# Making the first group of a max-unpooling kernel one image at a time

## The chip, the cores and the metric

The kernel runs on one core of a Trainium2 chip. The metric is the device time of one execution in microseconds (us), the median of several runs.

## The reference

A 2x2 max-unpooling: every input element goes to one of the four places of its 2x2 output block, chosen by an index from 0 to 3; the other three places are zero.

```
x: float32 [16, 64, 32, 32];  indices: int [16, 64, 32, 32], values 0..3
output[b, c, 2*i + idx // 2, 2*j + idx % 2] = x[b, c, i, j]     # else 0
```

The indices arrive as 64-bit integers, so the core reads 4.2 MB of x and 8.4 MB of indices and writes 16.8 MB.

## The kernel before

The 1,024 images lie on 128 partitions, eight images (t = 0..7) on each. Two images make a group; there are four groups, and each group is one store of 4 MiB. SyncE issues three loads, all on one queue: indices of images 0 to 2, all of x, indices of images 3 to 7. It then issues the four stores as VectorE signals them.

VectorE makes a piece of output with four instructions, one for each place in the 2x2 block: (index equals place) times x. Where it can, it treats two images in one instruction; images 2 and 3 are treated singly, because image 3 needs the second load of indices.

```
for t in range(T):                       # T = 8, G = 2, NG = 4, FIRST = 3
    g, k = t // G, t % G
    if t in (0, FIRST):
        ...                              # wait for this half of the indices
    if k == 1 and t != FIRST:
        continue
    n = 1 if k == 1 or t + 1 == FIRST else 2        # images per instruction
    if g == NG - 1:
        nc.vector.wait_ge(stored_0, 16)...          # group 3 reuses group 0's buffer
    ...
    for pidx in range(4):
        op = nc.vector.scalar_tensor_tensor(
            out=o_c[:, k : k + n, :, pidx // 2, :, pidx % 2],
            in0=idx_c[:, t : t + n], scalar=pidx, in1=x_c[:, t : t + n],
            op0=is_equal, op1=mult)
    if k + n == G:
        op.then_inc(made, 1)             # the group is made

for g in range(NG):
    nc.sync.wait_ge(made, g + 1)
    nc.sync.dma_start(out=out_v[g], in_=out_t[g]).then_inc(...)
```

Of the kernel before, what the change touches and what calls it, by code (L numbers as in the profile page):

```python
# [1 line left out]

# [4 lines left out]

P = 128
F32 = mybir.dt.float32
I32 = mybir.dt.int32  # L10


class Program:




    def __init__(self, nc):
        self.nc = nc
        self.block = nc.main_func.blocks[0]  # L20
        self.kernel_block = nc.cur_bb.bb.name

    def __enter__(self):
        ins = self.block.instructions
        self.branches = [i for i in ins if "Branch" in type(i).__name__]
        n = len(ins) - len(self.branches)
        assert all("Branch" in type(ins[k]).__name__ for k in range(n, len(ins)))
        del ins[n:]
        self.nc.switch_bb(self.block.name, parent=None)
        self.symbolic = self.nc._always_lower_symbolic_ap  # L30
        self.nc._always_lower_symbolic_ap = False
        return self

    def first(self, made):
        ins = self.block.instructions
        assert ins[len(ins) - 1].name == made.ins.name
        moved = ins.pop()
        at = next(
            k
            for k, i in enumerate(ins)  # L40
            if i.engine == moved.engine and isinstance(i, mybir.InstDrain)
        )
        ins.insert(at, moved)

    def last(self, made):


        def move(nc):
            ins = self.block.instructions
            at = next(k for k, i in enumerate(ins) if i.name == made.ins.name)  # L50
            nc.main_func.blocks[-1].instructions.append(ins.pop(at))

        self.nc.at_finalize(move)

    def __exit__(self, kind, *_):
        self.nc._always_lower_symbolic_ap = self.symbolic
        if kind is None:
            for b in self.branches:
                self.block.instructions.append(b)
            self.nc.switch_bb(self.kernel_block, parent=None)  # L60


@with_exitstack
def kernel(
    ctx: ExitStack,
    tc: tile.TileContext,
    x: bass.AP,
    indices: bass.AP,
    kernel_size: bass.AP,
    out: bass.AP,  # L70
):
    nc = tc.nc
    assert kernel_size == 2

    B, C, H, W = x.shape
    n_img = B * C
    T = n_img // P
    assert T * P == n_img and C % T == 0

    G = 2  # L80
    NG = T // G
    FIRST = 3
    N = H * W
    x_v = x.rearrange("b (ch t) h w -> (b ch) (t h w)", t=T)
    idx_v = indices.rearrange("b (ch t) h w -> (b ch) (t h w)", t=T).bitcast(I32)
    out_v = out.rearrange("b (ch g t) oh ow -> g (b ch) (t oh ow)", g=NG, t=G)

    x_t = nc.alloc_sbuf_tensor("x_t", [P, T * N], F32).ap()
    idx_t = nc.alloc_sbuf_tensor("idx_t", [P, T * 2 * N], I32).ap()
    out_t = [  # L90
        nc.alloc_sbuf_tensor(f"out_t{g}", [P, G * 4 * N], F32).ap()
        for g in range(NG - 1)
    ]
    out_t.append(out_t[0])

    x_in = nc.alloc_semaphore("x_in")
    idx_in = [nc.alloc_semaphore(f"idx_in{g}") for g in range(2)]
    made = nc.alloc_semaphore("made")
    stored_0 = nc.alloc_semaphore("stored_0")
    stored = nc.alloc_semaphore("stored")  # L100

    x_c = x_t.rearrange("p (t i j) -> p t i j", t=T, j=W)
    idx_c = idx_t.rearrange("p (t i j two) -> p t i j two", t=T, j=W, two=2)[
        :, :, :, :, 0
    ]
    cut = FIRST * 2 * N

    with Program(nc) as program:
        program.first(
            nc.sync.dma_start(out=idx_t[:, :cut], in_=idx_v[:, :cut]).then_inc(  # L110
                idx_in[0], 16
            )
        )
        program.first(nc.sync.dma_start(out=x_t, in_=x_v).then_inc(x_in, 16))
        program.first(
            nc.sync.dma_start(out=idx_t[:, cut:], in_=idx_v[:, cut:]).then_inc(
                idx_in[1], 16
            )
        )

        nc.vector.wait_ge(x_in, 16).then_inc(x_in, -16)
        for t in range(T):
            g, k = t // G, t % G
            if t in (0, FIRST):
                half = int(t == FIRST)
                nc.vector.wait_ge(idx_in[half], 16).then_inc(idx_in[half], -16)  # L126

            if k == 1 and t != FIRST:
                continue
            n = 1 if k == 1 or t + 1 == FIRST else 2  # L130
            if g == NG - 1:
                nc.vector.wait_ge(stored_0, 16).then_inc(stored_0, -16)
            o_c = out_t[g].rearrange(
                "p (m i two j wo) -> p m i two j wo", m=G, two=2, wo=2, j=W
# [4 lines that stand above are left out]
                    in0=idx_c[:, t : t + n],  # L139
                    scalar=pidx,  # L140
                    in1=x_c[:, t : t + n],
                    op0=mybir.AluOpType.is_equal,
                    op1=mybir.AluOpType.mult,
                )
            if k + n == G:
                op.then_inc(made, 1)

        for g in range(NG):
            nc.sync.wait_ge(made, g + 1)
            nc.sync.dma_start(out=out_v[g], in_=out_t[g]).then_inc(  # L150
                stored if g else stored_0, 16
            )
        nc.sync.sem_inc(made, -NG)
        program.last(
            nc.sync.wait_ge(stored, 16 * (NG - 1)).then_inc(stored, -16 * (NG - 1))
        )


# [1 line left out]
_INS = ['x', 'indices', 'kernel_size']  # L160
_OUTS = [((16, 64, 64, 64), 'float32')]

_NUMBERS = {'kernel_size': 2}


# [26 lines left out]
```

## Time and profile before

| | before |
|---|---|
| time, median of the first three runs | 71.51 us (71.4 to 71.56) |
| profiled span | 70.5 us |
| VectorE busy | 35.6 us, 20 instructions |
| transfer queue busy | 97.4% of 16 engines' span |
| first store issued | 28.60 us |
| first store packets start | 30.5 to 31.5 us |

The store is issued well before an engine can start on it, because each engine is still busy with load packets.

### The profile page before, as it was taken

What the parts mean: (1) busy time and instruction counts of PE and PEld (TensorE: products, weight loads), DVE (VectorE), ACT (ScalarE), POOL (GpSimd) and SP (SyncE); (2) the same over time, 40 slices, a digit from 0 to 9 for tenths busy, and PEclk for the clock granted to TensorE, in tenths of its full rate; (3) what the DMA queues carried; (4) which work ended last, traced back from release to release, by engine and by line L of the source; (5) the groups of instructions that cost most, each with busy time, mean ns of one, the idle gap of its engine ahead of it and who ended that gap; (6) DMA issues with size and microseconds to landing.
All of it is one profiled execution on the core that took longest, in us unless ns stands there. A gap on an engine that the chain in (4) does not pass through costs nothing.

```text
span 70.5 us, 72 instructions
## 1 busy us (share of the span) xinstructions
DVE 35.6 (51%) x20; POOL 0.2 (0%) x4
## 2 busy tenths in 40 slices
DVE  0000000000089999999999999999999300000000
POOL 1000000000000000000000000000000000000000
DMA  8799997979988999869898999989898989999891
GB/s 223 307 432 418 423 558 316 558 335 558 409 372 372 488 581 418 372 298 539 353 539 353 484 409 409 465 353 502 353 539 353 539 353 484 409 391 484 372 484 56
DMA packets 1008, 29.36 MB, mean 417 GB/s; under 512 B 112, under 2 KB 112, under 8 KB 112
## 3 DMA queue, kind: packets, MB, share of 16 engines
q1 hardware_dynamic: 1008, 29.36, 97.4%
HBM read 12.58 MB, written 16.78 MB: 417 GB/s over the span
## 4 chain that ended last, share of the span: by engine, by line
DVE 46%; DVEq 4%; issue 1%
DVE out_t L137 46%; DVEq L187 4%
## 5 line engine op out<-in xcount | busy, mean ns | idle before, releaser
L137 DVE SCALAR_TENSOR_TENSOR out_t<-idx_t,x_t 128x2048 f32<-128x2048 int32 (+1 forms) x20 | 35.6, 1860 | 19.7 <-DVEq L126 19.7
L173 POOL MEMSET const-bfloat16-1.0<- 128x1 bf16 x1 | 0.1, 103 | 0.0
L173 POOL MEMSET const-uint8-127<- 128x1 uint8 x1 | 0.1, 103 | 0.0
L173 POOL MEMSET const-float32-1.0<- 128x1 f32 x1 | 0.1, 100 | 0.0
L173 POOL MEMSET const-float32-0.0<- 128x1 f32 x1 | 0.1, 99 | 0.2 <-issue 0.2
## 6 DMA issues: line engine op xcount, KB each, us to landing
out_dram<-out_t SPq DMA_DIRECT2D x4, 4096.0 KB, 13.8
idx_t<-in_indices_dram SPq DMA_DIRECT2D x1, 5120.0 KB, 30.8
x_t<-in_x_dram SPq DMA_DIRECT2D x1, 4096.0 KB, 19.0
idx_t<-in_indices_dram SPq DMA_DIRECT2D x1, 3072.0 KB, 9.7
```

The costliest lines, as they stand in the source:

```text
L137: op = nc.vector.scalar_tensor_tensor(out=o_c[:, k : k + n, :, pidx // 2, :, pidx % 2], in0=idx_c[:, t : t + n], scalar=pidx, in1=x_c[:, t ...
L173: nc = _bacc.Bacc("TRN2", target_bir_lowering=False, num_devices=1)
L187: with _tile.TileContext(nc) as tc:
```

## The change

VectorE makes images 0 and 1 one after the other, as it does images 2 and 3. The diff isolates one effect: smaller instructions at the head of the work, and so a later issue of the first store.

```diff
-            if k == 1 and t != FIRST:
+
+            if k == 1 and t != FIRST and g:
                 continue
-            n = 1 if k == 1 or t + 1 == FIRST else 2
+            n = 1 if k == 1 or t + 1 == FIRST or not g else 2
```

## The prediction

> **What bounds the kernel now.** I read the views in this order: the page, to see which unit is full; the groups by shape, to get the price of one VectorE instruction; the chain of waits, to see when transfers land; and the trace cut into half-microsecond windows, to see whether the transfer engines ever lack work around the first store.
>
> The page of the kernel before:
>
> ```profile
> span 70.5 us, 72 instructions
> ...
> DVE 35.6 (51%) x20; POOL 0.2 (0%) x4
> ...
> DMA  8799997979988999869898999989898989999891
> ...
> q1 hardware_dynamic: 1008, 29.36, 97.4%
> HBM read 12.58 MB, written 16.78 MB: 417 GB/s over the span
> ```
>
> The reader should see that VectorE is busy for half of the span while the one transfer queue keeps 16 engines busy for 97.4% of it. The bytes are fixed by the problem: 12.58 MB in, 16.78 MB out. The first engine starts about 1 us after the first issue, so hardly any time is left in which the transfer engines are idle. The digits of the DMA row dip in places, but packets of this queue are 24 to 40 KB and are booked where they start, so single low digits are no proof of a gap. I need the waits for that.
>
> The chain of waits of the kernel before (start, length, what):
>
> ```profile
> 19.59 0.08 issue
> 19.67 12.07 DVE out_t L137 x7
> 31.74 0.15 issue
> 31.89 9.57 DVE out_t L137 x7
> 41.46 0.22 issue
> 41.69 2.57 DVEq L187
> 44.26 11.01 DVE out_t L137 x5
> ```
>
> This chain is VectorE's, but its breaks tell when transfers landed. At 19.6 x and the first three index images are there. At 31.7 VectorE resumes after its wait for the second part of the indices: the list of issues gives that load 30.8 us to landing, and it was issued at 0.90, so it landed at 31.7. At 41.4 comes the wait for the first store: the shortest issue-to-landing time of a store is 12.8 us, and 28.60 + 12.8 = 41.4. From the last load's landing to the first store's landing there are 9.7 us. A store is 4,096 KB, 4.19 MB; at 432 GB/s (what the windows show between 19.5 and 28.6, where the queue is certainly full) that is 9.7 us. So **there is no bubble between the last load and the first store**. Three more stores of 9.7 us from 41.4 give 70.5, the span. The whole kernel is about one microsecond of start and one uninterrupted string of transfers; VectorE runs beside it.
>
> The windows around the first store (window, length, DVE busy, POOL busy, clock, DMA share, GB/s), and the issue itself from the timeline:
>
> ```profile
> 29.50:30.00 0.50, 0.50 (x2) 0.00 (x0) 1.00 0.42 164
> 30.00:30.50 0.50, 0.50 (x1) 0.00 (x0) 1.00 0.00 0
> 30.50:31.00 0.50, 0.50 (x2) 0.00 (x0) 1.00 1.99 852
> 31.00:31.50 0.50, 0.50 (x1) 0.00 (x0) 1.00 0.46 197
> ...
> 28.60 0.35 SPq L150 DMA_DIRECT2D out_dram<-out_t  x1
> ```
>
> 852 GB/s in 0.5 us is 426 KB, which is 13 packets of 32 KB; 197 GB/s is 3 more. A row of out_t for two images is 32 KB, so these are the first store packets of all 16 engines: 13 start between 30.5 and 31.0, three between 31.0 and 31.5. The store was issued at 28.60. It therefore **sat in the queue for about 1.9 us or more**, behind the last load's 40 KB packets. That waiting time is what the change may eat.
>
> **What the Trainium skill says.** "VectorE: DVE Perf Modes", section on the TRN2 errata, says that instructions reading SBUF pay a fixed cost each, whatever their size, and gives (N+151)/0.96 ns for an fp32 instruction with two inputs: 2291 ns for 2048 elements, and 1224 for 1024. The trace agrees: 2286 and 1220 ns. "DMA: Bandwidth & Descriptors", section on queues, rings and completion order, says each engine consumes a queue's descriptors in ring order; the trace agrees, since a store issued at 28.60 starts only when the loads end. "Perfetto Trace Analysis", section on the HWDGE DMA instruction, says that the profiled window of such an instruction covers the issuing and not the movement of data; here the issue shows 0.35 us and the landing comes 12.8 us after its start.
>
> **The change part by part.** The loop now treats images 0 and 1 of group 0 one at a time. *Removed:* four instructions over 2048 elements. *Added:* eight over 1024. Groups 1 to 3 are made as before, and the signal for the first store still comes only with the last instruction of image 1, since it is given when k + n reaches 2. No bytes, buffers or transfers change. No wait is added: the second image needs nothing that the first did not.
>
> The cost comes from start-to-start distances, since successive VectorE records overlap a little at their ends. Two-image instructions: the timeline has the first at 19.67 and the third at 24.08, so 2.20 us each. One-image instructions: one starts at 31.89 in the chain, and the fourth after it (the last for image 3) at 36.43 in the timeline, so 4.54 us for four steps, 1.135 each. The groups by shape show the durations:
>
> ```profile
> L137 DVE SCALAR_TENSOR_TENSOR out_t<-idx_t,x_t 128x2048 f32<-128x2048 int32 x12 | 26.6, 2286 | 19.7 <-DVEq L126 19.7
> L137 DVE SCALAR_TENSOR_TENSOR out_t<-idx_t,x_t 128x1024 f32<-128x1024 int32 x8 | 9.2, 1220 | 0.0
> ```
>
> Group 0 now takes 8 x 1.135 = 9.08 us in place of 4 x 2.20 = 8.81, so **+0.28 us** on VectorE (four more fixed costs of 0.07 us). The first store is issued at 28.60 + 0.28 = 28.88 instead of 28.60.
>
> Does that reach the end? The deadline is the moment when the earliest engine runs out of load packets, between 30.5 and 31.0, less the time from an issue to the first packet. That time I take from the program's start: the first load is issued at 0.00, and the windows show no data in the first microsecond and full traffic in the second, so 1.0 us for the first engine; I allow 1.5 for the last. The store must be issued by about 30.5 - 1.5 = 29.0 at the most cautious, and by 29.5 at the likely figure. 28.88 meets both. The slack shrinks from about 0.9 to about 0.6 us by the likely figure. **The whole 0.28 us lies in the queue's waiting time: cost 0.**
>
> Later stores have more room. Store 1 is issued at 37.68 (timeline) and store 0 ends its transfer near 41.4, which leaves 3.7 us minus the 1.0 of issue; store 2 at 46.49 against 51.1; store 3 at 55.30 against 60.8. A shift of 0.28 in each changes nothing. VectorE even loses part of the shift, because it waits for the first store's landing at 41.4, which does not move, though it reaches this wait only just before that; I do not count on it. The sum is 71.5 + 0.0.
>
> **Rivals.** *First: the delay is passed on in full.* If the queue needs its descriptors earlier than I think (say 2 us before an engine runs dry, which no row here excludes for a store that reads SBUF), the 16 engines idle for up to 0.28 us between the last load and the first store, and every later landing shifts with it: 71.5 + 0.28 = 71.8, or +0.4%. Against it: before the change no time is lost at that joint, and the only issue latency on view is 1.0 us. *Second: VectorE becomes the bound.* It would have to lose the spare 2.7 to 4.5 us ahead of stores 1 to 3; 0.28 is too small. This would cost 0 as well. *Third: a gain.* Smaller instructions could finish an image earlier, but the store still waits for both, and the transfer queue is full anyway; nothing for it. *Fourth: VectorE's smaller instructions or a changed phase disturb the transfers.* Reads of SBUF by the store start while VectorE writes, as before; the engines move 431 to 446 GB/s in windows with either shape of instruction, so I see no effect of the shape.
>
> **How the range follows.** The best estimate is the median of before, 71.5. Its own three runs span 71.4 to 71.56; another chip or day may add a tenth or two on either side. The first rival adds 0.28 at about one chance in seven. The range is 71.3 to 71.8. Faster by over 2% would need 1.4 us out of a full queue: chance 0.01. Slower by over 2% would need five times the whole added VectorE time: 0.01. Within 2%: 0.98.
>
> **What would show each step right or wrong.** In the changed kernel the page should have 24 VectorE instructions, 16 of them over 1024 elements at about 1220 ns and 8 over 2048 at 2286, with VectorE busy near 35.9 us. The first store's issue should stand at about 28.9. The first store packets should still start in 30.5 to 31.5, with the issue-to-landing minimum down from 12.8 to about 12.5 us, and the chain should show the wait for the first store ending at 41.4 to 41.5 again. If instead that wait ends 0.2 us or more later while the last load still lands at 31.7, the store came too late for the queue and the first rival is right. The prediction would be wrong altogether if the one-image instructions were much dearer than 1.135 us when they are first on fresh data, or if the loads themselves ended earlier than in this trace, so that the slack was less than one profile shows.

## More of the kernel before

One reading aid for later: in a window, the DMA share books a packet's whole time where it starts. When each of the 16 engines starts exactly one packet in a window of 1 us, the DMA share is therefore the mean length of that packet in us.

## The result, and the profile after

| | before | after |
|---|---|---|
| time, median of six runs | 71.49 us (71.4 to 71.7) | 71.50 us (71.4 to 71.62) |
| ratio | | 0.9998 (95%: 0.9981 to 1.0015) |
| VectorE busy | 35.6 us | 35.9 us |
| x there, VectorE starts | 19.67 us | 19.56 us |
| first store issued | 28.60 us | 28.76 us |

A ratio is the mean time of one kernel's fast runs over that of the other's of the same rounds, so it is not quite the ratio of the medians quoted.

The page of the changed kernel, in the lines that answer to those of before:

```profile
span 70.2 us, 76 instructions
...
DVE 35.9 (51%) x24; POOL 0.2 (0%) x4
...
q1 hardware_dynamic: 1008, 29.36, 97.6%
```

The four more instructions and the 0.3 us of VectorE are there, and the queue is as full as before. The groups of the changed kernel by shape (busy us, then mean ns of one):

```profile
L138 DVE SCALAR_TENSOR_TENSOR out_t<-idx_t,x_t 128x1024 f32<-128x1024 int32 x16 | 18.3, 1219 | 19.6 <-DVEq L126 19.6
L138 DVE SCALAR_TENSOR_TENSOR out_t<-idx_t,x_t 128x2048 f32<-128x2048 int32 x8 | 17.7, 2283 | 0.0
```

The durations are those of before. The chain of waits of the changed kernel (start, length, what), up to the first store's landing:

```profile
19.56 11.92 DVE out_t L138 x11
31.48 0.57 issue
32.05 9.12 DVE out_t L138 x7
41.17 0.22 issue
```

The last load's landing is at 31.48 and the first store's at 41.17, 9.7 us apart, as before. (Both stand 0.26 to 0.29 us earlier than in the profile of before. That is not a gain of the change: VectorE's start, which the change cannot touch, is also earlier by 0.1, the profiled execution of before was 0.3 us over its median, and the timed runs of both kernels agree.) The issue of the first store (start, length, instruction; SPq is SyncE's queue), and the windows at the joint of loads and store, in the changed kernel:

```profile
28.76 0.35 SPq L151 DMA_DIRECT2D out_dram<-out_t  x1
...
30.50:31.00 0.50, 0.50 (x2) 0.00 (x0) 1.00 2.29 983
31.00:31.50 0.50, 0.50 (x2) 0.00 (x0) 1.00 0.15 66
```

983 GB/s in 0.5 us is 15 packets of 32 KB. All engines but one pass from loads to the store between 30.5 and 31.0, as soon as the loads end. VectorE's part from its start to the issue grew from 28.60 - 19.67 = 8.93 to 28.76 - 19.56 = 9.20 us, so by 0.27; all of it disappeared in the queue's waiting time.

### The profile page after: what moved, and what is told of

It is laid out like the page before. It is cut to its first block, busy times and chain, and to the rows that moved or that the text cites. A ratio compares the mean times of both kernels' runs of the same rounds, so it can differ in the third digit from the quotient of the medians.

```text
span 70.2 us, 76 instructions
## 1 busy us (share of the span) xinstructions
DVE 35.9 (51%) x24; POOL 0.2 (0%) x4
## 4 chain that ended last, share of the span: by engine, by line
DVE 46%; DVEq 4%; issue 1%
DVE out_t L138 46%; DVEq L188 4%
## 5 line engine op out<-in xcount | busy, mean ns | idle before, releaser
L138 DVE SCALAR_TENSOR_TENSOR out_t<-idx_t,x_t 128x1024 f32<-128x1024 int32 (+1 forms) x24 | 35.9, 1574 | 19.6 <-DVEq L126 19.6
## 6 DMA issues: line engine op xcount, KB each, us to landing
idx_t<-in_indices_dram SPq DMA_DIRECT2D x1, 5120.0 KB, 30.5
```

The lines of the kernel that those rows point to most:

```text
L138: op = nc.vector.scalar_tensor_tensor(out=o_c[:, k : k + n, :, pidx // 2, :, pidx % 2], in0=idx_c[:, t : t + n], scalar=pidx, in1=x_c[:, t ...
```

## The experiments

The time is the same, so the question is what makes it so: how much later could the store come, and does its issue matter at all? My theory was that each engine passes from its last load packet to its first store packet without a gap, as long as the store is issued some time ahead; beyond that each microsecond of delay costs one. The rivals were a queue that wants its work much earlier, and a time that does not depend on this issue at all. Each of the three calls of four runs shared its runs of the kernel before: 71.52, 71.49 and 71.50 us.

### Only the signal later, by one, two and three instructions

VectorE's work stays as it was before the change. Only the signal for group 0 moves onto an instruction of image 2 (number 1, 2 or 3), which is a clean dial for the issue time.

```diff
+                if (t, pidx) == (2, 0):          # (2, 1), (2, 2)
+                    op.then_inc(made, 1)
-            if k + n == G:
+            if k + n == G and g != 0:
                 op.then_inc(made, 1)
```

> The kernel before, with its ten or so microseconds of VectorE work unchanged; only the signal for the first store is moved from the last instruction of group 0 to the first instruction of image 2. The store is issued at about 28.60 + 1.14 = 29.73 us. Theory (the store has to be issued 1.0 to 1.5 us before an engine runs out of load packets, 30.6 to 31.4 us): this is just past the deadline, so the first engines stand idle; time +0 to +0.4 us (71.5 to 71.9). Rival 1 (the queue needs descriptors some 2 us ahead): +0.8 us or more. Rival 2 (the issue time of the first store is of no account within microseconds): +0.0.

> As the run before it, the signal two instructions later: the store is issued at about 30.87 us, when the first engines have run dry. Theory: the store packets can start only at 31.9 to 32.4, so the wait for the first store ends at about 42.4 instead of 41.4 and the time is 72.4 to 72.7 us (+0.9 to +1.2). Rival 1: +1.9 or more. Rival 2: +0.0 to +0.2.

> The kernel before with the signal for the first store three instructions later: issue at about 32.0 us. Theory (deadline 29.87, slope 1): +2.1 us, 73.6, slower by about 3%. Rival (only the step over the deadline costs, by a restart of the engines, not the length of the delay): +1.0 as in the run with the signal two later.

Measured: one later 71.58 us (ratio 1.0008, 0.9995 to 1.0022), two later 72.51 us (1.0139, 1.0125 to 1.0153), three later 73.68 us (1.0305, 1.0291 to 1.0319). The issue and the windows, first with the signal one later:

```profile
29.62 0.35 SPq L152 DMA_DIRECT2D out_dram<-out_t  x1
...
30.50:31.00 0.50, 0.50 (x2) 0.00 (x0) 1.00 2.29 983
```

Then with the signal two later:

```profile
30.86 0.35 SPq L152 DMA_DIRECT2D out_dram<-out_t  x1
...
30.50:31.00 0.50, 0.50 (x2) 0.00 (x0) 1.00 0.02 0
31.00:31.50 0.50, 0.50 (x1) 0.00 (x0) 1.00 0.00 0
31.50:32.00 0.50, 0.50 (x2) 0.00 (x0) 1.00 2.44 1049
```

And three later:

```profile
32.01 0.35 SPq L152 DMA_DIRECT2D out_dram<-out_t  x1
...
31.50:32.00 0.50, 0.50 (x2) 0.00 (x0) 1.00 0.00 0
32.00:32.50 0.50, 0.50 (x1) 0.00 (x0) 1.00 0.00 0
32.50:33.00 0.50, 0.50 (x1) 0.00 (x0) 1.00 2.43 1049
```

With the issue at 29.62 the engines still change over at the end of the loads. At 30.86 they have nothing to start between 30.5 and 31.5, and then all 16 start at once (1049 GB/s in half a microsecond is 16 packets). From issue to first packet that is 0.64 to 1.14 us by one run and 0.49 to 0.99 by the other. The single packets, which the kept traces hold though no view lists them, narrow it (windows of 0.05 us agree): the first engine starts 0.85 us after the issue and the last 1.0 us after it, with the signal two later as with three. The losses, 0.99 us at 30.86 and 2.19 at 32.01, grow by 1.20 for 1.15 us of delay. So the joint has a deadline near 30.86 - 0.99 = 29.87 us, and past it the loss follows the delay one for one. Both rivals fall: the issue time counts, and 2 us of lead are not needed. My own expectation of the first run was too pessimistic in its upper half; the lead of 0.85 to 1.0 us is shorter than the 1.0 to 1.5 us I had taken from the start of the program.

### The change carried further: half and quarter images

```diff
-            for pidx in range(4):
+            R = H if g else H // 2                # or H // 4
+            for pidx, r in [(p, r) for p in range(4) for r in range(0, H, R)]:
                 op = nc.vector.scalar_tensor_tensor(
-                    out=o_c[:, k : k + n, :, pidx // 2, :, pidx % 2],
+                    out=o_c[:, k : k + n, r : r + R, pidx // 2, :, pidx % 2],
                     ...                           # in0, in1 with r : r + R too
```

> The change carried one step further: group 0 in half images, 16 instructions over 512 elements. From the fixed cost of 0.07 us each, one takes 0.60 us and the group 9.63 instead of 8.81: the first store is issued at about 29.4 us, +0.83. Theory: at the likely deadline of 29.5, so +0.0 to +0.2 us. Rival 1 (2 us ahead): +0.5 or more. Rival 3 (many small instructions are dearer than the fixed cost says): the issue comes later than 29.6.

> The change carried further still: group 0 in quarter images, 32 instructions over 256 elements. Fixed cost 0.07 us each: 0.336 us from start to start, 10.75 us for the group, so the first store is issued at about 30.4 us. Theory after the first four runs (issues up to 29.6 are free; the run with the issue at 30.86 lost 0.99 us, so the joint's deadline is 30.86 - 0.99 = 29.87, and beyond it each microsecond of delay is one of time): +0.5 to +0.65 us (72.0 to 72.2). Rival (the issue time does not count, the loss of that run had another cause): +0.0.

Measured: halves 71.49 us (0.9999, 0.9987 to 1.0012), with the store issued at 29.52; quarters 72.26 us (1.011, 1.0096 to 1.0124). The issue with quarters, and the joint:

```profile
30.37 0.35 SPq L152 DMA_DIRECT2D out_dram<-out_t  x1
...
30.50:31.00 0.50, 0.50 (x1) 0.00 (x0) 1.00 0.02 0
31.00:31.50 0.50, 0.50 (x2) 0.00 (x0) 1.00 2.43 1049
```

Halves put the issue off by 0.92 us (0.82 counted from VectorE's start, which was 0.1 us later in this profile) and are still free. Quarters pass the deadline, the engines stand idle until 31.0, and the time grows. So the very thing that the change does has a cost, once there is enough of it. The size was a miss: 0.77 us against 0.5 to 0.65. Of this, 0.15 us is not in the span: for this kernel the time is 1.43 to 1.51 us longer than the span, against 1.27 to 1.38 for the others. The span itself grew by about 0.6 us, close to the 0.50 of the rule (30.37 - 29.87). What the extra time outside the span is was not tested; this kernel has the most instructions (100 in all).

### All groups one image at a time

```diff
-            if k == 1 and t != FIRST:
-                continue
-            n = 1 if k == 1 or t + 1 == FIRST else 2
-            if g == NG - 1:
+            n = 1
+            if g == NG - 1 and k == 0:            # still one wait for the buffer
```

> All images one at a time, in all groups: 32 instructions over 1024 elements, VectorE busy about 36.5 us. The later stores are issued 0.3, 0.55 and 0.83 us later than before. Theory: each has 2 us or more of room behind the store ahead of it, so the time is 71.5, +0.0. Rival (VectorE becomes the bound): +0.5 to +0.8 us.

Measured: 71.50 us (1.0004, 0.9991 to 1.0016), VectorE busy 36.4 us. VectorE is not the bound, and the later stores have the room that their times showed.

### The second store later

The same dial as in the first runs, for group 1: its signal moves to the first instruction of group 2, condition `(t, pidx) == (4, 0)`.

> The kernel before with the signal for the second store (group 1) one instruction of group 2 later: issue at 37.68 + 2.20 = 39.88 us. The engines finish the first store's packets 9.68 us after the loads', so by the same rule the deadline of this joint is 29.87 + 9.68 = 39.55. Theory: +0.3 us (+0.2 to +0.45), 71.8. Rival (the second store's issue is of no account, there is slack behind): +0.0.

Measured: 71.80 us (1.0047, 1.0035 to 1.006), +0.31 us, with the store issued at 39.77. The rule from the first joint gives 39.77 - 39.55 = 0.22 us for this issue; it holds at the next joint, where a store follows a store, to within 0.1 us. The slack there before was 39.55 - 37.68 = 1.9 us.

### Two stores for group 0, the first earlier

```diff
-        for g in range(NG):
-            nc.sync.wait_ge(made, g + 1)
-            ...
+        for t in range(G):
+            nc.sync.wait_ge(made, t + 1)
+            nc.sync.dma_start(out=half_v[:, t], in_=half_t[:, t]).then_inc(stored_0, 16)
+        for g in range(1, NG):
+            nc.sync.wait_ge(made, g + 2)
+            ...                                   # made also counts image 0
```

> The changed kernel, with its two images of group 0 stored by two transfers of 2 MiB, each as soon as its image is made: first issue at about 24.2, second at 28.9 us. Theory (the engines are full with loads until 30.6 anyway; an earlier issue only waits longer): +0.0. Rival (an earlier store lets the engines start stores beside loads, reads and writes of memory overlapping): -0.3 us or more. Small packets of 16 KB may cost up to +0.1.

Measured: 72.98 us (1.0202, 1.0185 to 1.022): slower by 1.49 us. Both theories were wrong; an earlier issue was not free but dear. The window in which each engine starts its last load packet, first in the changed kernel and then in this one:

```profile
29.00:30.00 1.00, 1.00 (x2) 0.00 (x0) 1.00 1.51 655
```

```profile
29.00:30.00 1.00, 1.00 (x2) 0.00 (x0) 1.00 2.50 655
```

Both windows hold the same 655 KB, 16 packets of 40 KB, one for each engine. Their mean length is 1.51 us in the changed kernel and 2.50 us with two stores. The loss arises in the loads, before any store packet starts.

This run changed two things, the time of issue and the number and size of the transfers. Four more runs took them apart. In the second and third of them the result is wrong: one whole store is signalled after two or three of the four instructions of images 0 and 1, and the rest write a spare buffer so that VectorE's times nearly stay (an instruction on the spare buffer took 2.44 us in place of 2.29). The last is their control.

```diff
# two stores, both late
-            nc.sync.wait_ge(made, t + 1)
+            nc.sync.wait_ge(made, 2)
# one whole store early (pidx > 1 with the signal at (0, 1); pidx > 2 with (0, 2))
+        nc.gpsimd.memset(out_t[0], 0.0).then_inc(zeroed, 1)
+        nc.vector.wait_ge(zeroed, 1).then_inc(zeroed, -1)
...
-                    out=o_c[:, k : k + n, :, pidx // 2, :, pidx % 2],
+                    out=spare_c[..., pidx % 2] if t == 0 and pidx > 1
+                    else o_c[:, k : k + n, :, pidx // 2, :, pidx % 2],
# control: the memset and its wait alone
```

> The kernel with two stores of group 0, but both issued only when both images are made, at about 28.8 and 29.2 us. It separates the two things that the run with two stores changed together, which lost 1.45 us where no change was expected; there the last packet of the loads took 2.3 to 2.6 us on every engine instead of 1.51. Theory A (the early issue does it: a store ready while an engine still has more than one load packet ahead delays the last of them): +0.0 to +0.2. Theory B (the 16 KB packets, or two issues in place of one, do it): +1.3 to +1.5, with the long last load packets again.

> Wrong result on purpose: the kernel before with one whole store of group 0, signalled after the second of the four instructions of images 0 and 1 (issue at about 24.2 us); the other two instructions write a spare buffer, so VectorE's times stay, and the rows that are missing are zeros set by GpSimd in the first microseconds. Theory A (early issue costs): +1.0 to +1.5, long last load packets. Theory B (split costs): +0.0.

> As the run before, signalled after the third instruction: issue at about 26.4 us, one instruction of the spare kind. Wrong result on purpose. Theory A: the store is ready at about 27.4, when each engine has one or two load packets left, so the same +1.0 to +1.5, or a part of it. Theory B: +0.0.

> Control for the two runs before: only GpSimd's setting of zeros and VectorE's wait for it are added, the store is issued at about 28.6 as in the kernel before, and the result is right. Both theories: +0.0. If it is slower, the two runs before have to be read against this one.

| run | first store issued | time | ratio (95%) |
|---|---|---|---|
| two stores, both late | 28.71 us | 71.59 us | 0.9993 (0.9954 to 1.0033) |
| whole store, 4 us early | 24.08 us | 72.91 us | 1.0169 (1.0127 to 1.0211) |
| whole store, 2 us early | 26.21 us | 72.96 us | 1.0179 (1.014 to 1.0217) |
| memset only | 28.45 us | 71.46 us | 0.9974 (0.9936 to 1.0013) |

The same window of the last load packets, for two stores late, and then for the whole store 2 us early:

```profile
29.00:30.00 1.00, 1.00 (x2) 0.00 (x0) 1.00 1.51 655
```

```profile
29.00:30.00 1.00, 1.00 (x2) 0.00 (x0) 1.00 2.69 655
```

Splitting costs nothing; the early issue does, with one transfer or two, and with right results or wrong ones. So the first store has a window: the issues tried at 24.1 to 26.2 us cost 1.4 to 1.5 us, issues from 28.45 to 29.62 are free, and from 30.37 on the delay is paid. Between 26.21 and 28.45 us nothing was tried, so where the early edge lies is open. What happens inside an engine when a store waits behind more than its last load packet is not shown; the runs show only that this last packet takes 2.5 to 2.7 us on average in place of 1.51. The single packets of the traces add that in the three early runs 8 to 14 of the sixteen packets just before the last were longer too (1.6 to 2.25 us) and no earlier load packet of that load was. So the cost did not grow with the lead between these two: 4 us early lost 1.41 us, 2 us early 1.46.

The kernel before may stand near the early edge of its window. In its profile the same window has a DMA share of 1.57 in place of 1.51, so some of its last load packets were longer, and two of its runs took 72.18 and 72.22 us, where none of the changed kernel's six passed 71.62. Its profiled execution, 0.3 us over the median, is the one with these longer packets. That is a hint and no more: those two slow runs left no trace to read, and the control with the memset, which issued earlier still (28.45 us), has no run above 71.66 us, though its window too shows 1.55.

No run beats the two kernels. All free variants end at 71.5 to 71.6 us, with the queue full.

## Why the prediction was right

**The bound.** The kernel is one unbroken string of transfers. The late-signal runs show it: once a gap is forced into the string, the time grows by about that gap, at the first joint and at the second. (With the signal two later, the single packets of the trace show each engine idle for 0.59 to 1.21 us between its last load and its first store packet; the time grew by 0.99.)

**The cost on VectorE.** Predicted +0.28 us to the issue; measured +0.27. Four more fixed costs of 0.07 us is the right account, and the same figure put the half and quarter images at 29.4 and 30.4 us (measured 29.52 and 30.37). The formula that the prediction takes from "VectorE: DVE Perf Modes" is stated there for `tensor_tensor`; that it fits the `scalar_tensor_tensor` of this kernel too is what the trace shows (2286 and 1220 ns).

**The slack.** Predicted about 0.9 us, of which 0.6 would be left; the deadline of 29.87 us makes it 1.27 before and 1.11 after. The estimate of the lead, 1.0 to 1.5 us from the first load of the program, was too long for a store in mid-run: 0.85 us for the first engine and 1.0 us for the last were measured. This erred on the safe side and did not change the forecast. For the second store the error went the other way: predicted 3.7 - 1.0 = 2.7 us, measured 1.9. The prediction counted from the landing of the first store at 41.4, but in the same trace the engines end its packets between 40.3 and 41.1 us, and what counts is when they run dry. The room was still ample for a shift of 0.28 us.

**The rivals.** The delay passed on in full: refuted by the result and by the run with the signal one later. VectorE as the bound: refuted by the run with all images single. Smaller instructions that disturb the transfers: not seen, since the same run, with all 32 of them small, has a ratio of 1.0004. An earlier store as a gain: I dismissed it because the queue is full, which is true, but the argument was incomplete; I took the queue's waiting time as free at any length, and the runs with an early issue show that too long a wait costs 1.4 to 1.5 us. The change moves the other way, so the forecast did not depend on it.

**Readings to correct.** The prediction says that VectorE "resumes after its wait" at 31.7. The chain marks the moment when the awaited load landed; VectorE was in the middle of an instruction then and never stood still. The same holds at 41.4: the wait for the first store was over there, but the first instruction that needs its buffer starts at 46.38. So VectorE loses no part of the shift, as the prediction thought it might; the issue of the last store moves by the same 0.16 us (55.30 to 55.46) as that of the first.

## What to carry to other kernels

Work beside a full transfer queue was free here up to a deadline: the moment when the engines run dry, less the time from issue to first packet (0.85 to 1.0 us here). Compare an added delay with that slack, and move the signal alone to test it. Do not assume that an earlier issue is always safe: here a store queued 2 us sooner behind the loads slowed their last packets and cost 1.46 us.

## What the Trainium skill lacked or had wrong

- "DMA: Bandwidth & Descriptors" has nothing on what a store costs that is queued behind loads too early, and its rules for kernel authors advise to issue a DMA early. Here an issue at 24.1 to 26.2 us in place of 28.4 or later lengthened the last 40 KB load packets from 1.51 to 2.5 to 2.7 us on average and the time by 1.4 to 1.5 us.
- The same page's specifications give a first-byte latency of about 0.6 us for this path. It does not say from which moment. From the start of the issue's record to the first packet the runs show 0.85 us on the first engine and 1.0 us on the last; from its end, 0.35 us later, 0.5 to 0.65 us.
